# A recurrence's value projection by Strassen's scheme, and weight copies that begin later

## The chip, the cores and the metric

The kernel runs on one core of a Trainium2 chip. The time is the device time of one execution in microseconds, the median of three runs. Five engines work side by side: TensorE (PE, with its weight loads PEld), VectorE (DVE), ScalarE (ACT), GpSimd (POOL) and SyncE (SP), which here only issues transfers. Each engine takes its instructions strictly in its own order and waits on semaphores where an operand isn't there yet.

## The reference

One layer with 512 tokens and a model width of 1024. A normalised input is projected by one wide matrix; its columns feed a gated linear recurrence (8 heads of 128 channels) and a latent attention (8 heads), and two gates merge both.

```python
h = rms_norm(x, norm_g[l])
proj = h @ w_in[l]
hq, hf, hi, hz, cq, ckv, kr, mz, glog = jnp.split(proj, pts, axis=-1)
y_a = hgrn2_branch(hq, hf, hi, hz, lower_bounds[l], hg_norm_g[l])   # values v = hi
y_b = mla_branch(cq, ckv, kr, mz, q_a_g[l], w_uq[l], kv_a_g[l], w_ukv[l])
merged = gates[:, :, 0] * (y_a @ w_proj_a[l]) + gates[:, :, 1] * (y_b @ w_proj_b[l])
x = x + merged @ w_out[l]
```

The change concerns `hi`, the recurrence's values: 512 tokens x 1024 inputs times 1024 inputs x 1024 columns.

## The kernel before

**Split products.** Every float32 operand of a large product is split into a high part (a cast to the matmul type, on ScalarE) and a low part (what the cast lost, a subtraction on VectorE). `mm3` then makes three matmuls of each pair: high x high, high x low, low x high. `load_w` does this for weights: a transfer of 512 KB into one of three raw buffers (`w_raw`), the cast (L129) into one of four high buffers, the subtraction (L130) into one of four low buffers.

**Stages.** The opening normalises `x` and turns it into `hT` (channels on partitions, high and low). Then come the latent projections (`c_second`, 96 matmuls of 448 columns) and four pairs of recurrence heads (`hg_pair`). A pair projects its forget gate F (`proj_ch`, 48 matmuls), its query Q (48) and its output gate ZA (48), and runs the scans and scores of its two heads (`hg_forget`, `hg_query`, `hg_scores`, `hg_out`). Pairs 0 and 2 project the values too, 512 columns each, for two pairs at a time (`proj_tok`, L606: 2 x 4 token blocks x 8 slices of 128 inputs x 3 matmuls of 512 columns). The eight attention heads follow, then the two gate products and the two output products.

**Block sums.** The gate product, the output projection of the recurrence and the final product run by Strassen's scheme in its form with seven block products of 256 tokens x 512 inputs x 512 columns, 24 matmuls each (`product`, `chain`, L895). They need sums of weight blocks and of token blocks. The weights' sums are made by transfers: SP's queue copies blocks inside HBM (32 copies, `BlockSums.start`), and POOL's queue later adds other blocks onto the copies with accumulating transfers (`add`, L803). The token sums S1 to S4 of `hT` are made in the first pair (`early_sums`, L826, L779, L783) in buffers that attention uses later, and saved in HBM (`h_dram`).

**What sets the order.** In a few stages TensorE's order is written by hand; elsewhere a scheduler with a timeline of its own orders each engine's instructions when the program is built. The copies wait in the list `queued`: each `load_w` takes one from it and issues it right behind its own load (`issue_after`). The additions wait in the list `adds`; `step` takes one at set places of a pair or of a head.

## Time and profile before

| | us |
|---|---|
| median of three runs | 606.92 (606.22 to 607.53) |
| profiled execution | 606.81 |
| its span | 605.0 |
| TensorE busy | 595.2 (98%) |
| VectorE busy | 430.1 (71%) |
| ScalarE busy | 282.1 (47%) |
| POOL busy | 159.5 (26%) |

The span is what the profiler saw of the program on the core; the execution's time is a little longer. A row of the timeline reads: start in us, duration in us, engine, line, operation, output<-input, shapes, count; in square brackets stands how long the engine had been idle and which instruction ended that. In a row of stretches each engine has its busy time and, after x, its instructions, in the order TensorE, weight loads, VectorE, ScalarE, POOL; then the granted clock, the share of the transfer engines and GB/s. Matmuls overlap: the row's 0.39 us for one of 512 columns is a modelled length, and successive ones start closer together.

### The profile page before, as it was taken

The page shows a single profiled execution, that of the slowest core. Times are in us where ns is not written, and L with a number is a line of the kernel's source. Part 1 is how long each engine was busy: PE and PEld are TensorE (multiplying, and loading weights), DVE is VectorE, ACT ScalarE, POOL GpSimd, SP SyncE. Part 2 cuts the span into 40 slices and gives each one's busy share as a digit, 9 for nine tenths or more (in the row PEclk, how much of TensorE's full clock was granted, in tenths as well). Part 3 has the DMA queues.
Part 4 walks back from the last instruction along what each step waited for, and adds up shares of the span by engine and source line. Part 5 has one row for each costly group of instructions (what it writes and reads, how often), then busy time and mean ns, then how long its engine had stood idle before and what let it go on. Part 6 is the DMA issues. An engine that isn't in the chain of part 4 may idle for free.

```text
span 605.0 us, 8841 instructions
## 1 busy us (share of the span) xinstructions
PE 595.2 (98%) x3198; PEld 501.4 (83%) x3198; DVE 430.1 (71%) x697; ACT 282.1 (47%) x517; POOL 159.5 (26%) x256
## 2 busy tenths in 40 slices
PE   8999999999999999999999999999999999999994
PEld 5998888888888888888888888888888888888884
DVE  6717988477654648768767686778878878466795
ACT  6555154333314332436555554456656764253553
POOL 3107602384460238524245440300000000000003
PEclk9999999999999999999999999999999999999998
DMA  8449579989889866772369676787666655467313
GB/s 274 157 141 334 171 251 381 261 168 278 209 175 273 174 198 119 186 148 65 68 156 169 153 157 158 203 301 244 190 193 202 196 186 187 134 225 262 105 36 139
DMA packets 73035, 115.34 MB, mean 191 GB/s; under 512 B 7560, under 2 KB 37662, under 8 KB 72992
## 3 DMA queue, kind: packets, MB, share of 16 engines
q1 hardware_dynamic: 63740, 90.99, 46.4%
q0 software_dynamic: 8336, 22.55, 20.8%
q10 hardware_dynamic: 916, 1.25, 0.6%
q8 instruction: 25, 0.41, 0.3%
q14 instruction: 18, 0.15, 0.1%
HBM read 106.38 MB, written 39.85 MB: 242 GB/s over the span
## 4 chain that ended last, share of the span: by engine, by line
PE 89%; DVE 4%; DMA 3%; ACT 2%; issue 1%; POOL 1%; SPq 0%; POOLq 0%; ACTq 0%; DVEq 0%
PE mm_ps L102 19%; PE mm_ps L104 19%; PE mm_ps L103 19%; PE ax_ps L895 16%; PE mm_ps L895 3%; PE ax_ps L760 1%; PE ax_ps L734 1%; DMA x<-x 1%; PE mm_ps L282 1%; PE ax_ps L562 1%; DVE ya L1179 1%; PE ax_ps L564 1%; PE ax_ps L524 1%; PE ax_ps L104 1%; PE ax_ps L103 1%
## 5 line engine op out<-in xcount | busy, mean ns | idle before, releaser
L130 DVE TENSOR_TENSOR w_lo<-w_raw,w_hi 128x1024 fp32r<-128x1024 f32 (+3 forms) x116 | 137.1, 1188 | 72.3 <-ACT w_hi L129 63.7
L129 ACT CAST w_hi<-w_raw 128x1024 fp32r<-128x1024 f32 (+3 forms) x116 | 114.6, 1006 | 124.5 <-PE mm_ps L103 59.4
L102 PE MATMUL mm_ps<-hT,w_hi 128*128 128x512 f32 x256 | 101.4, 396 | 0.0
L103 PE MATMUL mm_ps<-hT,w_hi 128*128 128x512 f32 x256 | 100.1, 391 | 0.0
L104 PE MATMUL mm_ps<-hT,w_lo 128*128 128x512 f32 x256 | 99.7, 392 | 0.0
L102 PE MATMUL mm_ps<-w_hi,hT 128*128 128x512 f32 (+1 forms) x160 | 61.7, 390 | 0.0
L103 PE MATMUL mm_ps<-w_lo,hT 128*128 128x512 f32 (+1 forms) x160 | 61.6, 386 | 0.0
L104 PE MATMUL mm_ps<-w_hi,hT 128*128 128x512 f32 (+1 forms) x160 | 61.4, 385 | 0.0
L102 PEld LDWEIGHTS mm_ps<-hT,w_hi 128*128 128x128 f32 x256 | 48.1, 188 | 9.8 <-DVE z L584 0.3
L104 PEld LDWEIGHTS mm_ps<-hT,w_lo 128*128 128x128 f32 x256 | 48.1, 188 | 9.8
L103 PEld LDWEIGHTS mm_ps<-hT,w_hi 128*128 128x128 f32 x256 | 48.1, 188 | 9.4
L895 PE MATMUL ax_ps<-w_hi,s 128*128 128x512 f32 x208 | 51.5, 390 | 0.0
L895 PEld LDWEIGHTS ax_ps<-w_hi,s 128*128 128x128 f32 x208 | 39.0, 188 | 8.1
L1196 POOL TENSOR_SCALAR ssum<-ssum 128x1 f32<-128x1 f32 x3 | 0.7, 225 | 163.3 <-ACT z L1183 163.2
L104 PEld LDWEIGHTS mm_ps<-w_hi,hT 128*128 128x128 f32 x160 | 30.1, 188 | 5.5
L102 PEld LDWEIGHTS mm_ps<-w_hi,hT 128*128 128x128 f32 x160 | 30.1, 188 | 5.3
L103 PEld LDWEIGHTS mm_ps<-w_lo,hT 128*128 128x128 f32 x160 | 30.1, 188 | 5.2
L742 ACT ACTIVATE p<-ax_ps,sm 128x128 f32<-128x128 f32 (+3 forms) x32 | 16.7, 525 | 35.2 <-DVE sm L741 35.0
L744 POOL TENSOR_SCALAR p<-p,sm 128x128 f32<-128x128 f32 (+3 forms) x28 | 15.6, 560 | 65.4 <-DVE sm L743 52.8
L895 PE MATMUL ax_ps<-w_lo,s 128*128 128x512 f32 x104 | 27.8, 389 | 0.0
L505 POOL TENSOR_TENSOR q<-qi,gh 128x256 f32<-128x256 f32 x8 | 6.9, 866 | 63.0 <-DVE qi L503 63.0
L895 PEld LDWEIGHTS ax_ps<-w_lo,s 128*128 128x128 f32 x104 | 19.5, 188 | 4.1
(323 smaller groups left out, 1210.1 us busy)
## 6 DMA issues: line engine op xcount, KB each, us to landing
w_raw<-w_in SPq DMA_DIRECT2D x54, 512.0 KB, 6.3
g_t<-w_in SPq DMA_DIRECT2D x16, 512.0 KB, 8.2
w_raw<-g_t SPq DMA_DIRECT2D x16, 512.0 KB, 4.9
g_t<-w_in POOLq DMA_DIRECT2D x8, 512.0 KB, 9.7
pa_t<-w_proj_a SPq DMA_DIRECT2D x8, 512.0 KB, 11.4
g_t<-g_t POOLq DMA_DIRECT2D x8, 512.0 KB, 10.4
out_t<-w_out SPq DMA_DIRECT2D x8, 512.0 KB, 6.3
s<-h POOLq DMA_DIRECT2D x8, 512.0 KB, 11.0
```

What stands on the lines that cost most here:

```text
L102: nc.tensor.matmul(ps, lh[lsl], rh[rsl], start=start, stop=False)
L103: nc.tensor.matmul(ps, lh[lsl], rl[rsl], start=False, stop=False)
L104: nc.tensor.matmul(ps, ll[lsl], rh[rsl], start=False, stop=stop)
L129: last_hi[0] = nc.scalar.copy(hi[:, :o], raw[:, :o])
L130: last_lo[0] = nc.vector.tensor_tensor(lo[:, :o], raw[:, :o], hi[:, :o].bitcast(F32), op=ALU.subtract)
L282: nc.tensor.matmul(ps, hT[l][:, 4 * kh + k, t * P : t * P + P], c_hl[kh][r][:, k * 256 : k * 256 + 256], start=kh == 0 and kind == 0 and k ...
L505: last_pool[0] = nc.gpsimd.tensor_tensor(c2_(q64), c4(qi)[:, :, 2:4], bc(gh, 10, 2), op=ALU.mult)
L524: nc.tensor.matmul(sps[:, sl], kt_[:, sl], v_sb[i][:, (h % 4) * P : (h % 4) * P + P], start=True, stop=True)
L562: nc.tensor.matmul(ops[:, sl], asb[:, sl], v_sb[i][:, (h % 4) * P : (h % 4) * P + P], start=True, stop=i == 0)
L742: last_act[0] = nc.scalar.activation(p[:, :n], sps[:, :n], AF.Exp, scale=SCALE, bias=sm[:, 1:2], accum_out=sm[:, 2:3])
L744: scaled_p = (nc.vector if final else nc.gpsimd).tensor_scalar(p[:, :n], p[:, :n], sm[:, 3:4], 0.5, op0=ALU.mult, op1=ALU.mult)
L895: nc.tensor.matmul(ps[:, o : o + n], ap[i][:, k, t * P : t * P + P], w[k // 2][j][:, k % 2, o : o + n], start=fresh and c == 0, stop=c == ...
```

## The change

The values become one product by the same seven-block scheme instead of two projections. With h11 to h22 for the halves of tokens and inputs, and w00 to w11 for those of the weights, the first pair makes five of the seven: h11 w00, S2 (w00 + w01 + w11), S3 (w01 + w11), h12 w10 and h22 (w00 + w01 + w11 + w10). They give the values of heads 0 to 3. The results of S2 and S3 that the other heads need are kept, negated, in four tiles of attention (`v_late`). Pair 2 makes S1 (w00 + w01) and S4 w11, and closes the values of heads 4 to 7.

The weight sums of the values don't go through HBM: w01 is loaded into a part of `ya` (the recurrence's result, unused until then; `x_sb` lies there too now), w11 is added by an accumulating transfer from POOL's queue, and VectorE adds w00 and w10. S2 and S3 are summed before the first pair and stay in SBUF until used (`early_sums`); S1 and S4 are summed behind pair 0 (`fetch_rest`). All four are still saved in HBM for the gate products. The gate and output weights' copies join the list only behind the first pair's values: eight entries (four saves of S2 and S3, four copies) go out at once, then one per load, and none in a few places (`behind`). The order of the additions is now plainly by weight, and the last two heads with a step take two each. Pair 2's output gate is now projected ahead of its query, as in pairs 1 and 3; a constant table (`qtab`) is loaded at the last pair, and pair 0 of the rope turns goes out on POOL's queue instead of ScalarE's.

```diff
+    def v_product(ap, w, done, banks=None, tile=ax_tile):
+        res = banks or [tile() for _ in range(2)]
+        for t, ps in enumerate(res):
+            for n, (x, k) in enumerate((x, k) for x in range(3) for k in range(4)):
+                i, j = ((0, 0), (1, 0), (0, 1))[x]
+                mm_ = nc.tensor.matmul(ps[:], ap(i, k, t), w[k // 2][j][:, k % 2], start=not banks and n == 0, stop=n == 11,
+                                       skip_group_check=banks is not None)
+            last_mm[0] = mm_
+            done(t, ps)
+        return res
...
+    for q in kh:
+        nc.sync.dma_start(i_w3[:, q], i_w[0, 1][:, q])
+    for q in kh:
+        nc.gpsimd.dma_start(i_w3[:, q], i_w[1, 1][:, q], accum_op=ALU.add)
+    for q in kh:
+        nc.sync.dma_start(i_w2[:, q], i_w[0, 0][:, q])
...
+    with tc.issue_after(c_lo_last.ins):
+        s_kept = early_sums()
+        for q in kh:
+            nc.vector.tensor_tensor(i_w2[:, q], i_w2[:, q], i_w3[:, q], op=ALU.add)
...
+    first_f = proj_ch(w_in, COL_F, hT)
...
+    first_u = v_product(h11, i_block(0, 0), first_values)
...
+    def values_first():
+        s2, s3 = [of_sum(s) for s in s_kept]
...
+        u = first_u
+        v_product(s2, i_split(i_w2), late(2), u)
+        v_product(s3, i_split(i_w3), late(3), u)
+        w10, raws = [], []
+        for q in kh:
+            w10.append(load_w(i_w[1, 0][:, q]))
+            nc.vector.tensor_tensor(i_w2[:, q], i_w2[:, q], last_raw[0].rearrange("p (k c) -> p k c", k=2), op=ALU.add)
+        v_product(h12, w10, lambda t, ps: nc.vector.tensor_tensor(v_sb[t][:], v_own[t][:], ps[:], op=ALU.add), tile=mm_tile)
+        v_product(h22, i_split(i_w2), lambda t, ps: nc.scalar.copy(v_sb[2 + t][:], ps[:]), u)
...
+        for w in (*gate_w, pa_w, out_w):
+            w.start()
+        with tc.issue_after(last_dma[0].ins):
+            for _ in range(8):
+                queued.pop(0)()
...
+    def values_rest():
...
+        r = v_product(of_sum(s_late[1]), i_split(i_w2), rest(3), tile=mm_tile)
+        v_product(of_sum(s_late[4]), i_block(1, 1), rest(2), r)
...
         if pair % 2 == 0:
             for t in range(NT):
                 v_sb[t] = hw.tile([P, 512], F32, f"v{t}")
-            proj_tok(w_in, COL_I + cc, hT, lambda t, ps: nc.scalar.copy(v_sb[t][:], ps[:]))
-        else:
+            (values_rest if pair else values_first)()
+        if pair:
             zz = gate()
...
-    adds = [(gate_w[0], 0), (gate_w[0], 2), (gate_w[1], 0), (gate_w[0], 1), (gate_w[1], 2), (gate_w[0], 3), (gate_w[1], 1),
-            (pa_w, 0), (gate_w[1], 3), (pa_w, 2), None, (pa_w, 1), (out_w, 0), (pa_w, 3), (out_w, 2), (out_w, 1), (out_w, 3)]
+    adds = [(gate_w[0], 0), (RestSum(),), (gate_w[0], 1), (gate_w[0], 2), (gate_w[0], 3), (gate_w[1], 0), (gate_w[1], 1),
+            (gate_w[1], 2), (gate_w[1], 3), None, (pa_w, 0), (pa_w, 1), (pa_w, 2), (pa_w, 3),
+            (out_w, 0), (out_w, 1), (out_w, 2), (out_w, 3)]
...
-            step()
+            for _ in range(1 + (h > 4)):
+                step()
```

`RestSum.add` (L723) adds w01 onto the second copy of w00 by an accumulating transfer, as L453 does with w11 in the opening.

The built order of VectorE ahead of the first pair, in the changed kernel. `e` are the whole token sums, `qn`, `kn`, `qp` and `qtab` the buffers of S2 and S3, `ya` holds the two weight sums; L132 is now the low part of a loaded weight:

```order
L174 TENSOR_TENSOR kn<-e_555,kn 128x512
L465 TENSOR_TENSOR ya<-ya 128x1024
L174 TENSOR_TENSOR qp<-e_557,qp 128x512
L174 TENSOR_TENSOR qtab<-e_557,qtab 128x512
L465 TENSOR_TENSOR ya<-ya 128x1024
L132 TENSOR_TENSOR w_lo<-w_raw,w_hi 128x1024 x3
```

Before, F's low parts stood behind the opening's small operations with no token or weight sum ahead of them; now they, the first two of the last row, stand behind both additions.

VectorE again, in the first pair, between the low parts of h12's weights (L132) and of h22's (L174 into `w_lo`); L734 and L300 are token sums of `fetch_rest`, L530 latent operands, L564 to L589 the first head's forget work, L705 the first value tile's sum:

```order
L132 TENSOR_TENSOR w_lo<-w_raw,w_hi 128x1024 x2
L174 TENSOR_TENSOR qn<-ya,qn 128x512
L530 SCALAR_TENSOR_TENSOR cT_92<-ax_ps,par,cT_91 128x512 x2
L300 SCALAR_TENSOR_TENSOR ya<-ya 128x512
...
L569 SCALAR_TENSOR_TENSOR pr<-f__763,fr 128x512
L300 SCALAR_TENSOR_TENSOR ya<-ya 128x512
L587 TENSOR_TENSOR ko<-k,tf 128x512
L572 RECIPROCAL inv<-pr 128x16
L174 TENSOR_TENSOR w_lo<-ya,w_hi 128x1024
...
L705 TENSOR_TENSOR v_845<-z,mm_ps 128x512
L174 TENSOR_TENSOR w_lo<-ya,w_hi 128x1024
```

Before, the first head's forget work stood ahead of the latent operands, and the token sums between the two heads' forget work.

POOL at heads 5 and 6 of attention, before and then in the changed kernel; `p` are the probabilities, whose scaling (L744, now L919) TensorE's transposes wait for:

```order
L803 DMA out_t3_659<-w_out 128x2x512 x2
L744 TENSOR_SCALAR p0_3693<-p0_3693,sm_3692 128x128
...
L803 DMA out_t2_658<-out_t1_657 128x1024 x2
L744 TENSOR_SCALAR p0_3860<-p0_3860,sm_3859 128x128
...
L803 DMA out_t4_660<-out_t2_658 128x1024 x2
```

```order
L973 DMA out_t1_785<-w_out 128x2x512 x2
L973 DMA out_t2_786<-out_t1_785 128x1024 x2
L919 TENSOR_SCALAR p0_3865<-p0_3865,sm_3864 128x128
...
L973 DMA out_t3_787<-w_out 128x2x512 x2
L973 DMA out_t4_788<-out_t2_786 128x1024 x2
```

The second sum of the output weights, which reads the first, stands right behind it now; before, a head's scalings stood between.

## The prediction

> **What bounds the kernel now.** I read the page's busy shares first, then who waited for whom on TensorE, then the chain of waits, then the timelines of the first pair. The page, and TensorE's waits at the weight loads, where a late operand shows:

> ```profile
> PE 595.2 (98%) x3198; PEld 501.4 (83%) x3198; DVE 430.1 (71%) x697; ACT 282.1 (47%) x517; POOL 159.5 (26%) x256
> ...
> PEld L247 <- issue: 2.2, 7, 0.5
> PEld L247 <- DVE zero L293: 1.2, 1, 1.2
> PEld mm_ps L282 <- ACT hT L273: 1.2, 1, 1.2
> PEld ax_ps L538 <- PE mm_ps L103: 0.7, 2, 0.4
> ```

> TensorE is busy for 98% of the span, and its longest wait for another engine in the whole run is 1.2 us, in the opening (L247, L282 stand before 26 us). No matmul of the recurrence waits for a load, a split or a copy that the view can name. So a matmul removed is worth its full pitch, and any new wait is paid in full. The pitch is read from the chain of waits, where whole products of the existing Strassen stages appear, and from the first pair's values on the timeline:

> ```profile
> 408.27 32.70 PE ax_ps L895 x144
> 440.97 5.44 PE mm_ps L895 x24
> ...
> 69.10 0.39 PE L102 MATMUL mm_ps<-w_hi,hT 128*128 128x512 f32 x1
> 69.33 0.39 PE L103 MATMUL mm_ps<-w_lo,hT 128*128 128x512 f32 x1
> ```

> One product of 24 takes 5.44 us, 0.227 us a matmul; the 0.39 is the modelled length of one, not its pitch. The values' own matmuls start 0.23 us apart.

> **What the change removes.** The values took 2 halves x 4 token blocks x 8 slices x 3 = 192 matmuls; seven products of 24 are 168. 24 x 0.227 = **5.44 us** go. They don't go where the work is: the first pair gets five products (120 matmuls for 96, 5.44 us more), pair 2 gets two (48 for 96, 10.88 us less).

> **What it adds, off TensorE.** Splits of value weights: 14 for 8.

> ```profile
> L130 DVE TENSOR_TENSOR w_lo<-w_raw,w_hi 128x1024 fp32r<-128x1024 f32 (+3 forms) x116 | 137.1, 1188 | 72.3 <-ACT w_hi L129 63.7 <-ACT osq L568 6.6 <-PE ax_ps L760 0.9
> L129 ACT CAST w_hi<-w_raw 128x1024 fp32r<-128x1024 f32 (+3 forms) x116 | 114.6, 1006 | 124.5 <-PE mm_ps L103 59.4 <-PE ax_ps L895 24.1 <-issue 10.8
> ```

> Six more are 7.1 us of VectorE and 6.0 of ScalarE. The four additions on the weights (L465, L704) are 1024 wide too: 4.8 us. The token sums were 24 operations of 512 columns and become 34 (early: three whole, three combinations of 1024 and four low parts; later 18): at 0.6 us, 6 us more. Six of the eight value tiles are now closed with a subtraction or an addition on VectorE: some 4 us. That is 22 us of VectorE in 605, at no cost except where TensorE waits for it. The early sums go where VectorE had nothing to do:

> ```profile
> 30.00:35.00 5.00, 5.00 (x27) 4.63 (x26) 0.97 (x5) 0.00 (x0) 0.00 (x0) 1.00 0.92 299
> 35.00:40.00 5.00, 5.00 (x26) 4.64 (x25) 0.00 (x0) 3.10 (x10) 0.00 (x0) 1.00 0.36 136
> 40.00:45.00 5.00, 5.00 (x26) 4.63 (x26) 1.83 (x2) 4.19 (x8) 0.00 (x0) 1.00 0.00 2
> ...
> 43.17 3.50 DVE L130 TENSOR_TENSOR w_lo<-w_raw,w_hi 128x1024 fp32r<-128x1024 f32 x3 [12.16 <-ACT w_hi L129]
> 45.49 0.53 ACT L400 COPY c_sb<-mm_ps 128x448 f32<-128x448 f32 x1 [0.17 <-PE mm_ps L104]
> ```

> VectorE (third pair of columns: busy, count) idles 12.16 us up to 43.17. Six operations of 1.14 us and four low parts of 0.6 are 9.2 us; begun at 30.6 they end near 40, and ScalarE's four casts (2.4 us) fit its gaps. The last c_kv product ends at 45.4, when F's product starts.

> **First place: F behind the sum of w01 and w11.** In VectorE's new order both L465 stand ahead of F's low parts, and each waits for an accumulating transfer from POOL's queue. What is queued behind them is F's low part, and TensorE's third matmul of F waits for that (45.4 + 0.45 = 45.9).

> ```profile
> 23.99 0.37 SPq L123 DMA_DIRECT2D w_raw<-w_in  x1
> ...
> L123 SPq DMA_DIRECT2D w_raw<-w_in x6: 367/372/379, 11.8 to 28.3; - x6
> DMA to landing us min/median/max: 3.7/4.5/6.2
> ...
> L803 POOL DMA_DIRECT2D g_t<-w_in x8: 1204/1474/1778, 102.6 to 169.6; - x8
> DMA to landing us min/median/max: 6.4/9.9/13.3
> ```

> Below the first row stand the loads issued before 30 us, and then the accumulating transfers of the whole run (issue, and landing). The new loads follow the issue at 23.99: the second goes out near 25 and is down by 31, at the longest of those landings. The accumulation then takes 6.4 to 13.3 us (into HBM; into SBUF the trace has none, so these rows are the bounds). The second sum lands at 37.4 to 44.3, 41 at the median; L465 ends at 42.1, F's cast at 43.8 and its low part at 44.9: no wait. At the longest F's low part is ready at 46.7, 0.8 us late. I take **0**, since the transfers move on queues that drop to 0.00 in 40 to 45 us. [...]

> **Second place: the fifth product (h22) behind VectorE.** TensorE by pitch: F 45.4 to 56.3, h11 to 61.7, twelve transposes (20 took 2.18 us) to 63.0, S2 to 68.5, eight transposes, S3 and h12 interleaved to 80.2, then h22. h22's weights may be split only when S3 has given up its two buffers; the eleventh matmul, at 80.2 + 10 x 0.227 = **82.5**, needs the second low part. VectorE's work from 68.6, when w10's first half is cast, to that split: four operations of 1024 (4.6 us), two scans (2.3), two cT parts (1.3), the forget gate and the reciprocal (0.6), eight of 512 (4.9), together 13.7 us: **82.3**. There is no margin. How it runs under such a load is seen in the same work before:

> ```profile
> 64.38 0.54 DVE L466 TENSOR_SCALAR f__635<-tf,c,c 128x512 f32<-128x512 f32 x1
> 64.84 0.68 DVE L826 TENSOR_TENSOR qr<-hT,hT 128x512 f32<-128x512 f32 x1
> ...
> 67.25 1.21 DVE L470 TENSOR_TENSOR_SCAN tf<-f__635,ends 128x512 f32<-128x512 f32 x1
> 68.38 0.66 DVE L172 TENSOR_TENSOR kpe<-ax_ps,kpe 128x512 fp32r<-128x512 f32 x1
> ...
> 72.75 0.69 DVE L491 TENSOR_TENSOR k<-ko,gh 128x512 f32<-128x512 f32 x1 [0.68 <-POOL gh L478]
> 73.97 1.11 DVE L172 TENSOR_TENSOR qp<-qs,qp 128x512 fp32r<-128x512 f32 x1
> 75.00 0.68 DVE L783 SCALAR_TENSOR_TENSOR qr<-qr,qh 128x512 f32<-128x512 f32 x1
> ...
> L467 POOL TENSOR_SCALAR fr<-f__635 x8: 709/1251/3512, 56.2 to 239.6; 128x16 f32<-128x16 f32 x8
> ```

> Starts lie 0.60 us apart for 512 columns and 1.13 for a scan. From 64.38 to 75.00 stand fifteen operations, 9.5 us by these pitches, and they took 10.6: 11% more, 0.68 of it a wait for POOL. 13.7 and 11% are 15.2: ready at 83.8, 1.3 us late. Without a wait 0; with POOL's `fr`, which the second scan waits for, at its longest (3.51 for 1.25), 3.5. I take **1.3**, the 11%, as it is the same work on the same engines. The time comes back nowhere: TensorE has no idle time to absorb it.

> **What follows is covered.** From h22's split to the first scores VectorE has 22.9 us by pitch, 25.4 with the 11%: done near 109.2; TensorE reaches them at 82.5 + 1.3 + 14 x 0.227 + 96 x 0.227 + 1.4 of small ones, about 110.2. Pair 2's splits read SBUF and are made 15 us before use. ScalarE is half idle. The copies of gate and output weights begin 23 us later, one per load, and the gate product that needs the first comes at 408. One new wait is on POOL: at head 5 the second output sum is issued right after the first, which it reads.

> ```profile
> 361.63 1.69 POOL L803 DMA_DIRECT2D out_t<-out_t  x2
> 376.41 0.82 POOL L744 TENSOR_SCALAR p<-p,sm 128x128 f32<-128x128 f32 x2 [13.09 <-DVE sm L743]
> 380.51 0.69 POOL L744 TENSOR_SCALAR p<-p,sm 128x512 f32<-128x512 f32 x1 [2.16 <-DVE sm L743]
> ```

> Issued at 361.6 and a little after, the first sum lands by 375.7 at the longest; with the issue POOL is free at 376.5. Head 6's scaling then waits behind it until 376.5 instead of 376.4, and its last piece is due at 380.5. Cost 0.

> **Sum.** -5.44 + 0 + 1.3 = -4.1. The profiled span of 605.0 becomes 600.9; the profiled execution's own time (606.81, 1.8 more than its span) 602.7, and as the median shown is 606.92, **602.8 us**. With the two bounds: 601.5 to 605.8.

> **Rivals.** *The stretch runs late twice (604.1 to 605.7).* If `fr` or a POOL product is slow for both heads, h22 loses 2.6 to 3.5 and Q or the scores up to 1 more: 606.9 - 5.4 + 2.6 to 4.2. For it: margins of 0 and about 1 us, and a row of 3.51. Against it: the same two heads lost 1 us together before. 17%.

> *The gain is eaten elsewhere (605.7 to 608.1).* The h22 wait at its longest with F 0.8 late and one more place of 1 to 3 us, for instance POOL at head 5, where each us beyond 379 costs one. Against it: head 5 needs a landing 3 us beyond the longest row. 12%.

> *VectorE becomes the bound of the first pair (611).* [...]

> ```profile
> 55.00:60.00 5.00, 5.00 (x33) 4.41 (x32) 4.36 (x7) 4.59 (x7) 3.60 (x8) 1.00 1.04 351
> 60.00:65.00 5.00, 5.00 (x25) 4.14 (x24) 5.00 (x10) 0.65 (x2) 2.63 (x7) 1.00 0.51 171
> 65.00:70.00 5.00, 5.00 (x23) 4.13 (x22) 5.00 (x7) 0.00 (x0) 3.51 (x1) 1.00 0.72 225
> 70.00:75.00 5.00, 5.00 (x24) 4.13 (x23) 4.32 (x9) 2.21 (x4) 4.29 (x10) 1.00 0.29 113
> ```

> POOL is busy for 14.0 of these 20 us, with the two heads' forget work that now falls between 72 and 96. If each of those stopped VectorE, its 36.6 us by pitch from 68.6 to the scores would be 50.6, over at 119.2 where an undelayed TensorE comes at 108.9: 10.3 lost against 5.44 won, 4.9 slower, 611.8; it decides where the pitch grows by 25% (9.1 us: 3.7 of slack and 5.4). The rows speak against it: VectorE was busy 18.7 of the same 20 us and lost 1.0 beside 14.0 of POOL. 10%. [...]

> **How the numbers follow.** The forecast, stalls of 0 to 2.6 us and so 601.3 to 604.1, has 61%. A measurement of this kernel tells about 0.2%, 1.2 us, from no change. Faster: 61 + 17 = 78%; within 0.2%: 12%; slower: 10%. The forecast's case, the first rival and part of the second make the range 601.2 to 606.0; below it only a removal of more than 5.44 us would lead, and nothing more is removed.

> **What would show it.** In the changed profile: 168 matmuls at the new product's line and 192 fewer at L102 to L104; TensorE's waits at the new product's line, for w_lo, in total 1 to 3 us, in the fifth product; none at F; VectorE without idle time between 68 and 100 us; the last pair's scores about 4 us earlier than before; POOL's second output sum at head 5 issued about 10 us after the first without a wait on TensorE behind it. I'm wrong if TensorE waits over 5 us in the first pair, if F's low part comes after 46 us, or if a copy or load is late in the gate products.

## The result, and the profile after

The changed kernel takes **611.4 us** (median of 11 runs, 607.1 to 615.0) where the kernel before takes 606.7 (11 runs, 606.2 to 608.5): a ratio of 1.007, 95% interval 1.0051 to 1.0089. It is 0.7% slower, and its runs spread over 8 us where those before spread over 2. The forecast was 602.8, with a range of 601.2 to 606.0. Two of six executions of one experiment (e11) took 2107 and 3391 us and are left out of its figures.

The matmuls went as forecast; the time went into waits. The page's line for the engines:

```profile
PE 593.1 (97%) x3174; PEld 498.3 (82%) x3174; DVE 452.3 (74%) x717; ACT 286.4 (47%) x523; POOL 173.1 (28%) x264
```

24 instructions fewer on TensorE, 22.2 us more on VectorE. By the removed work the span should be 605.0 - 5.4 = 599.6 us; it is 610.4 in the profiled execution (612.1 us, 0.7 above the median), so 10.8 us are lost. What TensorE waited for (total, times, longest):

```profile
PE ax_ps L622 <- ACT kt L614: 2.7, 1, 2.7
PE mm_ps L102 <- DVE z L682: 2.1, 1, 2.1
PE ax_ps L251 <- DVE zero L347: 1.2, 1, 1.2
PE ax_ps L1040 <- ACT part L1075: 1.1, 1, 1.1
PE ax_ps L636 <- DVE pr L602: 1.0, 1, 1.0
PE ax_ps L676 <- DVE k L668: 1.0, 1, 1.0
PE ax_ps L935 <- POOL p L919: 0.6, 1, 0.6
```

Before, only the wait for `zero` in the opening was over 0.7 us. The six new ones are 8.5 us, single waits at 254, 195, 426, 157, 238 and 318 us. None is in the first pair, where I had looked (no row of L478, the new product). Behind the longest comes a second loss. In these stretches (columns as in the prediction; the granted clock is the third number from the end) it is halved:

```profile
254.00:257.00 3.00, 0.58 (x3) 0.16 (x1) 0.58 (x1) 1.34 (x3) 0.00 (x0) 1.00 1.11 274
257.00:259.00 2.00, 1.70 (x14) 1.54 (x16) 1.86 (x4) 2.00 (x5) 0.36 (x1) 0.93 0.97 330
259.00:261.00 2.00, 2.00 (x32) 1.77 (x32) 1.97 (x3) 0.55 (x2) 1.93 (x3) 0.50 0.80 248
261.00:263.00 2.00, 2.00 (x50) 1.93 (x48) 1.97 (x5) 0.00 (x0) 0.00 (x0) 0.71 1.02 238
```

(0.07 + 0.50 + 0.29) x 2 us = 1.7 us of TensorE's work are lost to it. With the waits that makes 10.2 of the 10.8.

VectorE and ScalarE, which TensorE waited for, waited themselves. ScalarE's waits for transfers from the first pair's end to the fourth head, in the kernel before (one row, 105 to 325 us), then in the changed one (110 to 330 us):

```profile
ACT w_hi L129 <- DMA w_raw<-w_in: 0.7, 1, 0.7
```

```profile
ACT w_hi L173 <- DMA ya<-w_in: 10.8, 2, 9.4
...
ACT p L917 <- DMA w_raw<-w_in: 8.1, 1, 8.1
...
ACT w_hi L131 <- DMA w_raw<-w_uq: 7.4, 1, 7.4
...
ACT w_hi L131 <- DMA w_raw<-w_in: 5.0, 2, 3.9
...
ACT w_hi L131 <- DMA w_raw<-w_ukv: 3.7, 1, 3.7
```

Two cases show how such a wait reaches TensorE. **The first, at 157 us** (timeline of the second pair):

```profile
140.96 2.48 POOL L723 DMA_DIRECT2D ya<-w_in  x2
149.04 1.05 ACT L173 CAST w_hi<-ya 128x1024 fp32r<-128x1024 f32 x1 [9.44 <-DMA ya<-w_in]
150.00 0.59 ACT L596 ACTIVATE f__763<-mm_ps 128x512 f32<-128x512 f32 x1
...
156.99 1.14 DVE L602 TENSOR_TENSOR pr<-qi,inv 128x512 f32<-128x512 f32 x1
...
158.28 0.69 PE L636 MATMUL ax_ps<-pr,ko 128*64 128x64 f32 x16 [1.05 <-DVE pr L602]
```

The split of the late value weights, used at 169, stands in ScalarE's order ahead of the second pair's queries (L596). It waits 9.4 us for POOL's accumulating transfer, and the queries wait behind it. **The second, at 195 us** (third pair):

```profile
181.05 1.76 SPq L122 DMA_DIRECT2D w_raw<-w_uq  x3
183.64 1.72 POOL L973 DMA_DIRECT2D g_t<-g_t  x2
185.29 1.59 POOL L1006 DMA_DIRECT2D qtab<-c_qtab  x1
195.67 0.51 ACT L131 CAST w_hi<-w_raw 128x384 fp32r<-128x384 f32 x1 [7.36 <-DMA w_raw<-w_uq]
196.09 0.59 ACT L681 ACTIVATE z<-mm_ps 128x512 f32<-128x512 f32 x1
196.71 0.69 DVE L682 SCALAR_TENSOR_TENSOR z<-z,mm_ps 128x512 f32<-128x512 f32 x1
197.46 0.50 PE L102 MATMUL mm_ps<-hT,w_hi 128*128 128x512 f32 x1 [2.05 <-DVE z L682]
```

A load of 192 KB in three pieces, issued at 181, is still not there at 195. Behind its cast stand the gate's activations, which free TensorE's tile. POOL's addition L973 was issued 2.6 us after the load.

The longest wait, at 254 us, has the shape of the second: beside an addition a load of `w_ukv` is late, ScalarE's cast waits for it, and the copy `kt` behind the cast is what TensorE waits for.

```profile
243.87 2.49 POOL L973 DMA_DIRECT2D g_t<-w_in  x2
...
255.66 0.72 ACT L131 CAST w_hi<-w_raw 128x640 fp32r<-128x640 f32 x1 [3.65 <-DMA w_raw<-w_ukv]
...
256.78 0.85 ACT L614 COPY kt<-ax_ps 128x384 f32<-128x384 f32 x2
...
257.30 1.65 PE L622 MATMUL ax_ps<-v,kt 128*128 128x128 f32 x12 [2.72 <-ACT kt L614]
```

### The profile page after: what moved, and what is told of

Same layout as the page of the kernel before. It is cut to its first block, busy times and chain, and to the rows that moved or that the text cites. A ratio compares the mean times of both kernels' runs of the same rounds, so it can differ in the third digit from the quotient of the medians.

```text
span 610.4 us, 8818 instructions
## 1 busy us (share of the span) xinstructions
PE 593.1 (97%) x3174; PEld 498.3 (82%) x3174; DVE 452.3 (74%) x717; ACT 286.4 (47%) x523; POOL 173.1 (28%) x264
## 4 chain that ended last, share of the span: by engine, by line
PE 41%; DVE 5%; DMA 3%; ACT 3%; issue 2%; POOL 1%; ACTq 0%; POOLq 0%; DVEq 0%
PE ax_ps L1040 15%; PE mm_ps L102 6%; PE mm_ps L103 6%; PE mm_ps L104 6%; DMA w_raw<-w_in 3%; PE mm_ps L1040 3%; PE ax_ps L935 1%; DVE w_lo L132 1%; PE ax_ps L909 1%; DVE ya L1326 1%; ACT w_hi L131 1%; DMA w_raw<-w_out 1%; DVE s L174 1%; PE ax_ps L104 1%; PE ax_ps L103 1%
## 5 line engine op out<-in xcount | busy, mean ns | idle before, releaser
L132 DVE TENSOR_TENSOR w_lo<-w_raw,w_hi 128x1024 fp32r<-128x1024 f32 (+3 forms) x114 | 137.2, 1211 | 62.8 <-ACT w_hi L131 53.4
L131 ACT CAST w_hi<-w_raw 128x1024 fp32r<-128x1024 f32 (+3 forms) x114 | 112.6, 1005 | 135.8 <-PE mm_ps L103 35.7
L102 PE MATMUL mm_ps<-hT,w_hi 128*128 128x512 f32 x256 | 101.0, 395 | 2.1 <-DVE z L682 2.1
L103 PE MATMUL mm_ps<-hT,w_hi 128*128 128x512 f32 x256 | 100.2, 391 | 0.0
L104 PE MATMUL mm_ps<-hT,w_lo 128*128 128x512 f32 x256 | 99.4, 392 | 0.0
L102 PEld LDWEIGHTS mm_ps<-hT,w_hi 128*128 128x128 f32 x256 | 48.1, 188 | 12.2 <-DVE z L682 2.5
L104 PEld LDWEIGHTS mm_ps<-hT,w_lo 128*128 128x128 f32 x256 | 48.1, 188 | 9.8
L103 PEld LDWEIGHTS mm_ps<-hT,w_hi 128*128 128x128 f32 x256 | 48.1, 188 | 9.5
L102 PE MATMUL mm_ps<-w_hi,hT 128*128 128x512 f32 (+1 forms) x96 | 36.9, 388 | 0.0
L104 PE MATMUL mm_ps<-w_hi,hT 128*128 128x512 f32 (+1 forms) x96 | 36.5, 382 | 0.0
L103 PE MATMUL mm_ps<-w_lo,hT 128*128 128x512 f32 (+1 forms) x96 | 36.5, 382 | 0.0
L919 POOL TENSOR_SCALAR p<-p,sm 128x128 f32<-128x128 f32 (+3 forms) x28 | 15.6, 562 | 51.5 <-DVE sm L918 28.6
L102 PE MATMUL mm_ps<-cT,w_hi 128*128 128x512 f32 x52 | 20.6, 396 | 0.0
L104 PEld LDWEIGHTS mm_ps<-w_hi,hT 128*128 128x128 f32 x96 | 18.0, 188 | 3.1
L104 PE MATMUL mm_ps<-cT,w_lo 128*128 128x512 f32 x52 | 20.4, 392 | 0.0
```

The source lines that it names most:

```text
L102: nc.tensor.matmul(ps, lh[lsl], rh[rsl], start=start, stop=False)
L103: nc.tensor.matmul(ps, lh[lsl], rl[rsl], start=False, stop=False)
L104: nc.tensor.matmul(ps, ll[lsl], rh[rsl], start=False, stop=stop)
L131: last_hi[0] = nc.scalar.copy(hi[:, :o], raw[:, :o])
L132: last_lo[0] = nc.vector.tensor_tensor(lo[:, :o], raw[:, :o], hi[:, :o].bitcast(F32), op=ALU.subtract)
L919: scaled_p = (nc.vector if final else nc.gpsimd).tensor_scalar(p[:, :n], p[:, :n], sm[:, 3:4], 0.5, op0=ALU.mult, op1=ALU.mult)
```

## The experiments

The theory after the first reading (T): transfers of the gate and output weights delay the loads beside them. Rivals: the scheme's own 22 us of VectorE (W), the late begin of the copies, the shortened third pair, ScalarE's order. All times are medians of 4 to 11 executions; before measured 606.5 to 606.9 beside each run. A trace is one execution, which can lie off its median (e2's took 616.7 us). e1, e5, e11, e12 and e17 leave sums out, so their values aren't the reference's.

| kernel | us | ratio to before |
|---|---|---|
| changed | 611.4 | 1.0051 to 1.0089 |
| e1 no copies, no additions | 601.75 | 0.9902 to 0.9932 |
| e2 copies early | 612.8 | 1.0072 to 1.0148 |
| e3 before, copies and additions late | 609.6 | 1.0028 to 1.0062 |
| e4 split held | 607.2 | 0.9988 to 1.0041 |
| e5 no additions | 602.0 | 0.991 to 0.9943 |
| e6, e7 split held, no copies in pair 2 | 607.2, 607.1 | 0.9996 to 1.0017, 0.9992 to 1.0019 |
| e8 third pair 48 matmuls longer | 619.8 | 1.0193 to 1.023 |
| e9 copies early, additions at old places | 612.8 | 1.0078 to 1.0123 |
| e10 = e9 with split held | 603.3 | 0.9936 to 0.9969 |
| e11 six additions beside the second to fourth pair out | 603.7 | 0.9944 to 0.9972 |
| e12 eight additions of the heads out | 607.9 | 1.0012 to 1.0051 |
| e14 split held, copies early | 612.0 | 1.0061 to 1.0098 |
| e15 split held, old places, copies late | 609.9 | 1.0038 to 1.0073 |
| e16 = e14, one addition a stage later | 606.4 | 0.9975 to 1.0003 |
| e17 = e14, one addition out | 603.4 | 0.9931 to 0.996 |
| e13 = e10 with POOL's order changed | **602.0** | 0.9907 to 0.9932 |

### e1: no copies, no additions

```diff
...
-            self.t = [dram.tile([P, 4, 512], F32, name=f"{name}_t{n}") for n in range(1, 5)]
+            self.t = [self.w[ij] for ij in TERMS]
...
-            for t, ij in zip(self.t, TERMS):
-                for q in kh:
-                    queued.append(...)
+            return
...
-            if x:
+            if x and isinstance(x[0], RestSum):
```

> The changed kernel without the 32 copies and the 16 additions of the gate and output weights: the Strassen products of those weights read plain blocks of the weights in place of the sums, so the values are not the reference's and the matmuls are as many as before. Theory T (transfers): in the changed kernel's trace TensorE waits 2.4 us at 197.5, 3.1 at 254.3, 0.6 at 286, 0.9 at 318.5 and 1.4 at 427.5, each behind a cast on ScalarE whose weight load came late (3.7 to 7.4 us of waiting for a load), because copies and additions of weights are still running beside the loads of pair 2 and later. Then these 8.4 us go: 611.4 - 8.4 = about 603, and the 1.2 us at 158.3 (ScalarE waiting for the value weights' own accumulation) and perhaps the 1.35 at 238 stay. Rival W (work): the 22 us of additional VectorE and POOL work of the new scheme itself makes the stages late; then the time stays at 609 or above.

601.75 us: nearly all of the loss is gone; the removed matmuls alone would give 606.5 - 5.4 = 601.1. W falls: the new work on VectorE (451.3 us busy here, 430.1 before) costs TensorE some 0.7 us. Even the wait at 157 is gone: ScalarE still stands in the late split's cast, but for 5.3 us in place of 9.4, and that the queries can bear.

### e2: copies begun early

```diff
+    for w in (*gate_w, pa_w, out_w):
+        w.start()
     first_f = proj_ch(w_in, COL_F, hT)
...
-        for w in (*gate_w, pa_w, out_w):
-            w.start()
-        with tc.issue_after(last_dma[0].ins):
-            for _ in range(8):
+        with tc.issue_after(last_dma[0].ins):
+            for _ in range(4):
```

> The changed kernel with the copies begun where the kernel before begins them, with the first load of the recurrence's forget weights, one per load; the order of the additions is the changed kernel's. Theory T with the late start as its cause: the copies are over about 23 us earlier, no copy of the output weights is left for the heads, and of the 8.4 us of late loads 5 or more go: 603 to 606. Rival D (demand): the stages of pair 2 and 3 are shorter by 11 us of TensorE's time and their loads and additions do not shrink, so the loads come late wherever the copies begin: 609 to 612. If the first pair's own loads then come late, its waits show before 110 us and the time is above 611.

612.8: no gain, nearest to rival D. The late begin of the copies, taken alone, isn't the cause. The gate's wait in the third pair was 3.6 us in the profiled execution.

### e3: the kernel before with late copies and additions

```diff
             proj_tok(w_in, COL_I + cc, hT, lambda t, ps: nc.scalar.copy(v_sb[t][:], ps[:]))
+            if not pair:
+                for w in (*gate_w, pa_w, out_w):
+                    w.start()
+                with tc.issue_after(last_dma[0].ins):
+                    for _ in range(4):
+                        queued.pop(0)()
```

together with the changed kernel's list of additions, its places and `behind`.

> The kernel before with this part of the change alone: copies begun behind the first pair's value loads, additions in the changed kernel's order and at its places, no Strassen for the values. Theory T with the late start as its cause: the late loads of pair 3 and the heads appear here too, 2 to 6 us: 609 to 613. Rival D or W: without the new products nothing is late, 606.5 to 607.5.

609.6, 3.1 more than before: this part of the change costs time in the old kernel too, with no Strassen product of the values. So the transfers' timetable has a price of its own. The forecast named late loads of the fourth pair and the heads, though, and TensorE's new waits in the trace stand elsewhere: 1.1 us at 136 us, for the second pair's gate, and 0.5 at 423. The changed kernel's loss is larger, 611.4 - 601.1 = 10.3 us.

### e4: the late split held back

```diff
-        r = v_product(of_sum(s_late[1]), i_split(i_w2), rest(3), tile=mm_tile)
+        with tc.issue_after(last_act[0].ins), tc.issue_after(last_dve[0].ins):
+            w_rest = i_split(i_w2)
+        r = v_product(of_sum(s_late[1]), w_rest, rest(3), tile=mm_tile)
```

> The changed kernel with ScalarE's and VectorE's split of the late value weights issued behind the last query and turn work of the second pair, no longer ahead of it. In the changed kernel ScalarE stands 9.4 us in the first of these casts until the accumulating transfer has landed at 149.0, the second pair's queries wait behind it, and TensorE waits 1.2 us at 158.3 for a score operand. Theory S (ScalarE's order): that wait goes, 1.2 us: 610.2, the other waits stay. Rival: the queries were late for VectorE's or POOL's sake, and 611.4 stays, with a wait of about 1 us at the second pair's scores.

607.2: 4.2 us, where theory S had 1.2 and the wait itself was 1.0. It is gone, and the gate's wait shrank to 1.3 us, the one at 254 disappeared; a new one of 2.1 us stands at 272. The waits seem to hang together, since the third pair's loads follow the second pair's splits; no run divides them.

### e5: copies, but no additions

```diff
-            if x:
+            if x and isinstance(x[0], RestSum):
```

> The changed kernel with the 32 copies but without the 16 additions to them (the accumulation of the value weights stays), so the Strassen products of the gate and output weights read the copied block in place of the sum and the values are not the reference's. Without copies and additions the time was 601.75, 9.7 below the changed kernel. If the additions, which move 6 to 8 MB through the slower queue at 9 us each, are what delays the loads, nearly all of that goes: 602 to 604. If the copies, issued right behind the loads on the same queue, are, little goes: 608 to 611. If both count by their bytes, half: 606 to 607.

602.0, 0.2 from e1. Without the additions the 32 copies cost nothing; **the 16 additions cost 9.4 us**. T holds, narrowed to the additions. (They are 32 transfers of 512 KB, 16.8 MB, more than the 6 to 8 MB of the expectation.)

### e6, e7: no copies in the third pair

Both hold the split. e6 takes two copies per load in the first two pairs and none in the third; e7 also two per load in the fourth.

```diff
             for _ in range(8):
                 queued.pop(0)()
+        behind[0] = 2
...
-        if pair == 3:
+        if pair == 2:
             behind[0] = 0
```

> The changed kernel with the late split held back as in the run before it, and with the copies taken two per load in the first two pairs, none in the third, and one per load after. In the changed kernel the transfers are without a gap from 175 to 205 us (the third pair, with seven copies), and stand still for much of 115 to 125, 155 to 160 and 170 to 175. Theory D (the third pair's transfers don't fit its shortened time): the wait of 2.4 us at 197 goes, against the kernel with the held split alone (607.2) 1.5 to 3 us are won: 604 to 606. Rival: the additions alone fill that stretch, no gain: 607.

> The run before it with two copies per load also for the fourth pair's forget and gate weights, where the transfers of the changed kernel stand still from 222 to 240 us; six copies are left for the heads, where it was ten. Theory D: the loads of the fourth pair's end and the first heads come earlier, another 1 to 2 us: 603 to 605. Rival: the additions issued from 238 on are what those loads wait for: no gain over the run before it.

607.2 and 607.1: as e4, though the third pair's gate waits in neither (the wait of 0.8 us of the same form stands at 274 and 277). Taking the copies out of the third pair wins nothing in the whole; other waits came in place (in e7 1.8 us at the pairs' scores and 1.6 at the fourth pair's outputs).

### e8: a longer third pair

```diff
-        r = v_product(of_sum(s_late[1]), i_split(i_w2), rest(3), tile=mm_tile)
+        r = v_product(of_sum(s_late[1]), i_split(i_w2), rest(3), tile=mm_tile, times=3)
```

> The changed kernel with the first late product's 24 matmuls issued three times into the same bank (only the last pass counts), so that the third pair has 48 matmuls more, as many as the scheme took out of it: 10.9 us of TensorE at the pitch of 0.227, and not one transfer more. Theory D: the transfers bound this pair and the next, so the waits at 197 and 254 and the half-clock stretch behind the second (2.4, 3.1 and about 1.7 us) shrink and the time grows by 4 to 7 us only: 615 to 618. Rival (the loads are late for the order in which queues and engines take them, whatever the pair's length): the full 10.9: 622.

619.8, 8.4 more for 10.9 us of work: neither forecast. The third pair's gate waits no longer (0.8 us of this form stand at 289), the wait at the fourth pair's turn fell to 0.3, and the clock stayed whole, but new waits came (1.5 us in the opening among them, where nothing was changed). Some 2.5 us of the loss hang on how short the pair is; by theory D, with the transfers' total as the bound, 4 to 7 would have come back.

### e9, e10: additions at the old places

```diff
-    adds = [(gate_w[0], 0), (RestSum(),), (gate_w[0], 1), (gate_w[0], 2), (gate_w[0], 3), (gate_w[1], 0), ...
+    adds = [(gate_w[0], 0), (gate_w[0], 2), (RestSum(),), (gate_w[1], 0), (gate_w[0], 1), (gate_w[0], 3), ...
...
-        if pair:
-            step()
+        step()
         kts = [hg_turned(k[5]) for k in kk]
...
-            for _ in range(1 + (h > 4)):
-                step()
+            step()
```

on top of e2; e10 has the held split as well.

> The changed kernel with copies begun as early as in the kernel before and with the additions at the kernel before's places (a first one in the first pair's query stage, one per head, not two, in the last heads) and nearly its order; the accumulation of the value weights stands in the third place. Without the additions the changed kernel took 602.0, with early copies alone 612.8. Theory P (places): the additions cost what they cost because of where the change put them; at the old places the late loads go: 603 to 606. Theory Q (order in the shorter pairs): the additions hang on POOL's last operation of each stage, and with the third pair 11 us shorter they and the loads of pairs 3 and 4 fall together whatever the list says: 608 to 613.

> The run before it with the late split held behind the second pair's query and turn work, which alone was worth 4.2 us (611.4 to 607.2). Under theory P 602 to 604, better than both kernels; under theory Q 604 to 608, no more than the held split is worth.

612.8, where theory Q had it, and 603.3, where theory P had it. Early copies and old places alone win nothing, the held split alone 4.2, all three 8.1. e10 beats both kernels and is 0.5 from the forecast of 602.8.

### e11, e12: which additions

```diff
-            x = adds.pop(0)
-            if x:
+            n, x = 18 - len(adds), adds.pop(0)
+            if x and not 3 <= n < 9:
```

(10 to 18 in e12)

> The changed kernel without the six additions that are issued from 174 to 260 us (the second pair's end to the fourth pair's queries); the Strassen products that read them get the plain copies, so the values are not the reference's. The waits at 197 (2.4) and 254 (3.1, and 1.7 by the halved clock behind it) stand beside these additions. Theory A (the additions delay the loads beside them): 611.4 - 7.2 = 604, the waits at 158, 238 and in the heads stay. Rival: the loads are late for the copies and the other transfers of that stretch, 608 or more.

> The changed kernel without the eight additions in the heads (projection and output weights), values not the reference's for the same reason. Theory A: only the waits from 286 on go (0.6, 0.9 and 1.4 us, together 2.9): 608.5, and the gain of this run and of the run before it, 2.9 and 7.2, add up to about the 9.4 us that all additions cost. Rival: most of the cost lies in the heads, where two additions stand behind one head: 605 or less.

603.7 and 607.9: 7.7 us lie with the six additions beside the second to the fourth pair (7.2 was forecast), and 3.5 with the eight in the heads. Their sum, 11.2, is more than the 9.4 of e5; the runs of the changed kernel spread too far to tell these apart.

e12 is the changed kernel up to the heads, yet its profiled execution has no wait for the gate at 195: it issues the load of `w_uq` at 181.4 and the addition at 183.9, as far apart as in the changed kernel's, and casts at 189.8 instead of 195.7. So whether this load comes late differs from one execution to the next, which fits the changed kernel's spread of 8 us.

### e14, e15: which two of three

e14 is e4 with e2; e15 is e4 with e9's list and places, its copies late and two per load in the first two pairs.

> The changed kernel with the held split and with copies begun as early as in the kernel before; the additions at the changed places and in the changed order. Theory C (the copies' begin is what the held split needs): 603 to 604. Theory P (the additions' places are): as the held split alone, about 607.

> The changed kernel with the held split and the additions at the kernel before's places and in nearly its order; the copies begin behind the first pair's value loads as in the changed kernel, two per load up to the second pair's end so that each is there before its addition. Theory P: 603 to 604. Theory C: about 607.

612.0 and 609.9: neither C nor P. All three are needed for 603; the held split with only one of the others is worse than alone (607.2). In e14 nearly everything stands in one wait, the one for the gate's tile:

```profile
PE mm_ps L102 <- DVE z L725: 5.4, 1, 5.4
```

(L725 is L682 of the changed kernel.) So the question became why the load of `w_uq` lands by 187.9 in e10 and after 195 in the changed kernel and e14. e10's timeline, then e14's:

```profile
180.65 1.41 SPq L122 DMA_DIRECT2D w_raw<-w_uq  x3
182.59 0.89 POOL L522 DMA_DIRECT2D g_t<-g_t  x1
...
187.86 0.51 ACT L131 CAST w_hi<-w_raw 128x384 fp32r<-128x384 f32 x1 [1.26 <-DVE w_lo L132]
```

```profile
180.96 2.69 SPq L122 DMA_DIRECT2D w_raw<-w_uq  x3
182.90 1.79 POOL L522 DMA_DIRECT2D g_t<-g_t  x2
...
198.20 0.51 ACT L131 CAST w_hi<-w_raw 128x384 fp32r<-128x384 f32 x1 [9.58 <-DMA w_raw<-w_uq]
```

The issues differ by 0.3 us, the casts by 10.3. What the queues moved from 188 to 193 us (q1 has the loads and copies, q0 POOL's transfers; packets, MB, share of the 16 engines), first before, then the changed kernel, then e14, then e10:

```profile
q1 hardware_dynamic: 1579, 1.29, 89.4%
```

```profile
q0 software_dynamic: 245, 0.92, 90.3%
q1 hardware_dynamic: 383, 0.23, 17.7%
```

```profile
q0 software_dynamic: 192, 0.72, 85.8%
q1 hardware_dynamic: 208, 0.14, 13.7%
```

```profile
q0 software_dynamic: 240, 0.88, 86.0%
q1 hardware_dynamic: 209, 0.21, 15.3%
```

Beside POOL's transfers the load queue moves a sixth to a ninth: 208 packets beside 192 in e14, about one for one. In e10 it moves no more; there the load of `w_uq` is already through, and the loads behind it have time. The load is 768 packets of 256 bytes, 48 for each of the 16 engines if they are spread evenly. In e10 the trace has all of them through by 187.4. In e14 31 run between 188 and 189 and 8 to 22 in each of the next seven microseconds; in the changed kernel 733 are through by 189, and then come three to five a microsecond from 189 to 195. In the kernel before, the addition of this stage was issued at 174.8, its last packets ran at 184, and the load was issued at 184.8: they missed each other.

The changed kernel's last 35 packets, fewer than one engine's share, show how they are held up. From 189.3 to 193.7 us most of them start 0.33 or 0.34 us apart, while the addition's packets of 4096 bytes take 0.33 us each. Then they start 0.17 us apart, while those of the table `qtab` (0.16 us each) follow in POOL's queue, and from 195.0 on 0.015 us. By these spacings one of them went through for each packet of POOL's, and the load waits for the last of them. That they lie on a single engine and pass one for one is an estimate from their number and spacing; the trace doesn't name the engine.

What differs ahead of the load is more than the 0.3 us of its issue: the addition before it. That one, issued at 171.3 in e10 and at 171.9 in e14, has its last packets at 182.3 in e10 (from a copy, in packets of 4096 bytes) and at 185.9 in e14 (from `w_in`, in packets of 2048). The next addition's first packets follow at 185.6 and 186.1; by 187, 740 of the load's 768 packets are through in e10 and 459 in e14.

### e16, e17: one addition moved, one left out

In e14, `step` behind the third pair's forget gate goes to its query (e16), or its addition is left out (e17, `not 4 <= n < 5`).

```diff
-        if pair:
+        if pair and pair != 2:
             step()
         def gate():
...
         if pair:
-            step()
+            for _ in range(1 + (pair == 2)):
+                step()
         kts = [hg_turned(k[5]) for k in kk]
```

> Held split and early copies (612.0 in the run before), with one addition issued a stage later: the one that hangs on the third pair's forget work goes behind its query work, together with the one that is there. In that run's profile TensorE waits 5.4 us at 199.9 for the gate's tile and its clock is then halved for 6.8 us, 3.4 lost: together 8.8. Theory M (the small load meets this addition): all of it goes, 603.2; up to 605 if the two additions at the query work make another load late. Rival (the additions' places in the pair before, or the clock, decide): 610 or more, with the wait at 200 still there.

> The same kernel with this one addition left out (the fourth sum of the first gate half lacks its second block, so the values are not the reference's). The load of the query table, 512 KB, still follows in its queue. Theory M: 603.2, the wait at 200 and the halved clock gone. Rival: 610 or more.

603.4 without that one addition, as theory M had it: **one addition of sixteen cost 8.6 us**. From 188 to 193 the load queue has its rate back:

```profile
q1 hardware_dynamic: 1314, 1.43, 88.2%
q0 software_dynamic: 37, 0.12, 6.5%
```

Of the 8.6, the wait is 5.4. Behind it e14's stretches show the clock at half:

```profile
196.00:198.00 2.00, 0.00 (x0) 0.00 (x0) 0.00 (x0) 0.00 (x0) 0.00 (x0) 0.92 1.00 310
198.00:200.00 2.00, 0.01 (x1) 0.02 (x1) 1.18 (x2) 1.48 (x3) 0.00 (x0) 0.50 1.06 373
...
204.00:206.00 2.00, 2.00 (x9) 1.64 (x8) 0.02 (x1) 1.05 (x1) 0.00 (x0) 0.87 0.95 266
```

TensorE works again from 200, so 4 x 0.5 + 2 x 0.13 = 2.3 us are lost to it. The expectation's 8.8 counted the whole of the halved time, though TensorE stood still in the first part; 0.9 us stays unexplained. Moved a stage later (e16) the same addition gives 606.4, 1.4 more than theory M allowed: the gate's wait is gone, and a wait for the third pair's output grew, with a halved clock behind it:

```profile
PE ax_ps L719 <- DVE k L711: 2.6, 1, 2.6
```

That one, 1.0 to 1.1 us in most kernels, is not from transfers: it stood in e1 and e5 as well.

### e13: POOL's order

```diff
-        with tc.issue_after(last_pool[0].ins):
+        with tc.issue_after(last_pool[0].ins), tc.issue_after(last_ss[0].ins):
             nc.gpsimd.tensor_tensor(qr[:], qr[:], qtab[:, 0], op=ALU.mult)
```

in e10; `last_ss` is the last normalisation of a pair's outputs.

> Early copies, old places and held split as in the kernel that took 603.3, and POOL's rotation of the first two heads' queries (three operations of 512 columns, 1.3 to 2.3 us each) issued behind the third pair's normalisation (two of 4 columns), no longer between its halves. In that kernel TensorE waits 1.1 us at 235 for an output that waits for this normalisation. Theory: the wait goes, 602.2. Rival: the rotated queries, the addition issued ahead of them and the forget work behind them come later and the same microsecond is lost in the fourth pair: 603.3 or more.

602.0, ratio 0.9919 (0.9907 to 0.9932), five runs between 601.6 and 602.3: **the best of the kernels that compute the reference**. The time is what theory gave, but that is luck: the wait was to go, and the profile still has it, longer.

```profile
PE ax_ps L719 <- DVE k L711: 1.6, 1, 1.6
```

The span is 0.7 shorter than e10's all the same. Where that came from was not followed up.

## Where the prediction was right and wrong

**The sum's first term, -5.44, was right.** e1 gives 601.75 with the new products and no transfers of the other weights, 4.8 under its own before; e5 4.8, e13 4.9.

**F behind the weight sums: 0, right.** TensorE has no wait there.

**The fifth product: 1.3 us forecast, 0 measured.** The changed kernel's timeline has its second low part (L174) done at 82.1, 1.7 us earlier than I had worked out, and no wait of TensorE at L478:

```profile
80.86 1.22 DVE L174 TENSOR_TENSOR w_lo<-ya,w_hi 128x1024 fp32r<-128x1024 f32 x1
```

The planned order there held; my 11% for slow operations was too much.

**The rival in which VectorE becomes the bound of the first pair (611.8) gave the right time for a wrong reason**: its place, the first pair, has no wait at all, and e1 keeps nearly all of VectorE's added work at 601.75. Its term, VectorE stopped for as long as POOL is busy, is shown by no run: in the changed kernel h22's second low part was done at 82.1, 0.2 us ahead of the 82.3 worked out with VectorE never stopped.

**The step that failed is "What follows is covered"**, three sentences of it. *Pair 2's splits are made 15 us before use*: so they were, but the first waits for an accumulating transfer, and I didn't name what is queued behind it on ScalarE: the second pair's queries. I had done this for VectorE at F and not here. *ScalarE is half idle*: true on average (47%), and worthless to queries that stood behind a cast which waited 9.4 us. *The copies begin 23 us later, and the gate product needs the first at 408*: I asked whether a copy or sum would be late for its own use. None was. What I didn't ask is which loads stand beside the additions. (One of them came late in the gate product too: ScalarE waited 2.9 us for a load of `w_in`, TensorE 1.1 us at 426, the last of the prediction's signs of being wrong.) The term that I took as 0 measured 9.4 us (611.4 against 602.0), most of it (7.7 in e11) beside the second to fourth pair. What the additions cost in the kernel before was not run; its waits, 2.1 us in all and in the opening, leave them little. "The gain is eaten elsewhere" was the right heading at 12%, but the place I named in it, POOL at head 5, cost TensorE nothing: the second sum was issued at 375.1 and 379.5, and the scaling behind it was in time.

**The last pair's scores** begin at 258.9 where I forecast 4 us earlier than 257.4; that sign showed the error.

What stays open: that the addition ahead decides whether the load of `w_uq` gets through was read from packets, and not tried by itself. The held split's 4.2 us were not divided between its own wait and the loads that follow. And why the additions' cost by parts (11.2) is more than in one (9.4) isn't known.

## What to carry to other kernels

When a change shortens a stage, list the transfers that are issued in it and beside it, not only their bytes: an average share below one says nothing about two transfers that meet. Give a load whose cast stands ahead of other work its own time away from accumulating transfers (the addition beside the load of `w_uq` cost 8.6 us, e14 against e17), and hold a cast of late data behind the work that is ready (4.2 us, e4). Where a kernel's runs spread more than before the change, look for such a meeting first.

## What the runs showed of the hardware

**Beside accumulating transfers the load queue moved little.** From 188 to 193 us it moved 1.29 MB before, 0.23, 0.14 and 0.21 beside POOL's transfers (changed kernel, e14, e10), and 1.43 with one addition left out (e17). In the changed kernel an addition's packet of 4096 bytes took 0.33 us, a plain one of that size (`qtab`) 0.16. That one packet of a load goes through for each of POOL's is my estimate, from 208 packets beside 192 in e14 and from the spacing of the changed kernel's last 35, 0.33 to 0.34 us beside POOL's packets of 0.33. By this estimate a load in small packets gets the fewest bytes; no run changed a load's packet size to test that.

**After some waits of under 3 us TensorE's clock was halved.** After waits of 2.7 us (changed kernel) and 2.6 us (e16) the granted clock was 0.50 for about 3.4 us; after 2.1 us at 195 in the changed kernel it stayed at 1.00, while 2.1 us at 272 in e4 were followed by 0.50 as well, again for about 3.4 us. e16's stretches:

```profile
238.00:240.00 2.00, 1.55 (x7) 1.39 (x8) 2.00 (x4) 0.60 (x1) 2.00 (x5) 0.68 0.66 150
240.00:242.00 2.00, 2.00 (x6) 1.61 (x5) 2.00 (x4) 0.00 (x0) 2.00 (x5) 0.50 1.19 185
242.00:244.00 2.00, 2.00 (x10) 1.58 (x10) 0.55 (x1) 0.00 (x0) 2.00 (x6) 0.97 0.98 180
```
